# A hybrid attention and DeltaNet layer on one core: new prices for the kernel's own instruction order, decay columns in two products, squares summed by TensorE, softmax sums by transposes

## The chip, the core and the metric

The kernel runs on one core of a Trainium2 chip. The core has five engines with a queue each, executed in order: TensorE (PE; its weight loads are shown apart as PEld), VectorE (DVE), ScalarE (ACT), GpSimd (POOL) and SyncE (SP), which here only issues DMA transfers. The metric is the device time of one execution in microseconds (us).

## The reference

One layer of a diffusion backbone over 512 latent tokens and 256 context tokens of width 1024, in float32:

```python
mod = silu(c) @ w_ada + b_ada                    # 6 x 1024: shift, scale, gate, twice
mod_c = silu(c_ctx) @ w_ada + b_ada              # the same for the context
h  = rms_norm(x, g_norm1) * (1 + sc1) + sh1      # 512 x 1024
hc = rms_norm(ctx, g_norm1) * (1 + csc1) + csh1  # 256 x 1024
aq, ak, av, dq, dk, dv, dz, da, db, ga, gd = split_cols(h @ w_in)   # and of hc @ w_in
y_attn = window_ctx_attention(...)               # 8 heads, window 128, all context keys, a sink
beta = sigmoid(db); g = -exp(a_log) * softplus(da + dt_bias)        # decay columns
o_d = bidir_delta(...)                           # gated DeltaNet, both directions, chunks of 64
y = sigmoid(ga) * (y_attn @ w_br_attn) + sigmoid(gd) * (norm(o_d) * silu(dz) @ w_br_dn)
x = x + gt1 * (y @ w_out)
x = x + gt2 * (square(relu((rms_norm(x, g_norm2) * (1 + sc2) + sh2) @ w_mlp1)) @ w_mlp2)
```

## The kernel before

Channels lie on the 128 partitions and tokens in the free dimension. A float32 product of good accuracy is made of three fast ones: each operand is split into an upper part (rounded by an ACT copy, line 279 for weights and 211 or 308 for features) and the rest (a DVE subtraction, lines 284, 212, 309), and `mm3` issues upper x upper, upper x rest and rest x upper (lines 301, 302, 303); `gate_tiles` does the same on line 1048, and the MLP on line 1517. A weight tile is 128 output columns of all 1024 inputs, 512 KB, in eight k-parts.

**The early stage.** TensorE first runs 30 warm-up products (`NONES`, line 217). x and ctx are loaded whole. `ada(kt)` loads two 512 KB blocks of modulation weights and multiplies them with the condition (line 236, 32 columns wide on the array); `columns(kt)` turns the rows into per-channel scale and shift (lines 252, 257, 265, 266). `norm1` squares x on ACT (line 327), sums four tiles on DVE (lines 333 and 337) and multiplies the sum by ones (line 340) to get the norm; `features(kt)` applies norm, scale and shift (lines 307 to 309), for x and ctx together. Three input tiles, T_AB (the decay columns `da` and `db`: 64 columns that are used, 64 of zeros), T_DK and T_DK + 1, are held in PSUM and fed k by k as the features come; `columns` runs two k ahead (`AHEAD`).

**The rest.** The decay columns become per-chunk decay factors (lines 705 to 763; first used by the products of line 742). Attention has eight units (block of queries, kv head): `scores`, then `outputs`, which transposes the probabilities (line 621), multiplies by the values (lines 610 and 611) and scales with the reciprocal sums, spread over partitions by four f32 products with the identity (line 642). The DeltaNet inverts 32 x 32 blocks on DVE, combines them (lines 893 to 904) and runs a chain of chunk steps in both directions (`chain_step`, lines 1164, 1183, 1203, 1221), whose products use 64 x 64 quadrants of the array. Gate tiles (line 1048) and branch tiles (line 1094) are emitted between as fill. The MLP takes the second half of the time.

**The order.** What is emitted isn't the order of execution. `arrange` takes all instructions with their dependencies (`needs`) and simulates the engines: an engine that is free takes, of the instructions that are ready, the one emitted first. The simulated order is then fixed for every engine, DMA issues on SP and POOL among them. `Step.cost` gives the time that an operation holds its engine and the time until its result is there; `SIGNAL`, 120 ns, is added for a consumer on another engine.

Of the kernel before, what the change touches and what calls it, by code (L numbers as in the profile page):

```python
# [30 lines left out]
AHEAD = 2  # L31
# [5 lines left out]
SIGNAL = 120  # L37
# [30 lines left out]
T_AK, T_AV, T_AQ, T_AB = 0, 1, 2, 6  # L68
T_DK, T_DV, T_DQ, T_DZ = 7, 11, 15, 19
T_GA, T_GD = 23, 31  # L70
N_IN = 39
# [44 lines left out]
def tile_layer(ctx: ExitStack, tc: tile.TileContext, I: dict, out: bass.AP, dbg=None):  # L116
# [25 lines left out]

    def cload(key, shape, pool=const):
        t = pool.tile(list(shape), F32, name=f"c_{key}")
        nc.sync.dma_start(out=t, in_=I[key])
        return t
# [11 lines left out]
    ties = []  # L158

# [46 lines left out]
    def follow(later, earlier):  # L206

        tie(later.ins, earlier.ins.name)
# [19 lines left out]
    def ada(kt):  # L228


        rp_ = banks.get(512, True)
        for half in range(2):
            wb = alloc(1024)
            nc.sync.dma_start(out=wb.ap, in_=I["wada1"][kt, half])
# [3 lines left out]
            wb.free()  # L238
        return rp_
# [47 lines left out]
    early, EARLY = [], {T_AB: 0, T_DK: 0, T_DK + 1: 0}  # L287
    ebufs = []

    def load_early():  # L290
        bb = alloc(1024), alloc(1024)
        ebufs.extend(bb)
        early.append((wload(I["win"][list(EARLY)[len(early)]], bufs=bb), bank(2)))


    def mm3(acc, w, xs, start=True, stop=True, ks=None):
        ks = list(range(len(xs))) if ks is None else ks
        n = len(ks)
        for i, k in enumerate(ks):
            xhi, xlo = xs[i]  # L300
            PE.matmul(acc, w[0][:, k, :], xhi, start=(start and i == 0), stop=False)  # L301
            PE.matmul(acc, w[0][:, k, :], xlo, start=False, stop=False)  # L302
            r = PE.matmul(acc, w[1][:, k, :], xhi, start=False, stop=(stop and i == n - 1))  # L303
        return r
# [10 lines left out]
    w0 = upper[0]  # L315
# [33 lines left out]
    def features(kt):  # L349

        t = alloc(768)
        o, oc = kt * 1024, kt * 512
        if len(hx) == kt:
            hx.append(modulate(t[:, :512], xt[kt], rx, modA[:, kt, 0:1], modS[:, kt, 0:1],
                               H[:, o:o + 512], H[:, o + 512:o + 1024]))
        if len(normed) == 2:
            hc.append(modulate(t[:, 512:768], ct_[kt], rc, modA[:, kt, 1:2], modS[:, kt, 1:2],
                               HCb[:, oc:oc + 256], HCb[:, oc + 256:oc + 512]))
        t.free()
# [5 lines left out]
    normed = [norm1(xs_, 4, SEQ, rx)]  # L365
    follow(w0, normed[0])
    columns(0, rp0)
    features(0)
    hi0 = upper[0]
    columns(1, ada(1))  # L370
    load_early()
    low0 = early_x(*early[0], 0)
    follow(low0, last[0])
    last[0] = low0
    normed.append(norm1(cs_, 2, CTX, rc, hi0))
    for kt in range(KT):
        features(kt)
        if kt + AHEAD < KT:
            columns(kt + AHEAD, ada(kt + AHEAD))
        if len(early) < len(EARLY):  # L380
            load_early()
        for (w, acc), k0 in zip(early, EARLY.values()):
            for k in range(kt + 1) if kt == k0 else (kt,):
                if k or acc is not early[0][1]:
                    early_x(w, acc, k)
                mm3(acc[:, 512:768], w, [hc[k]], start=(k == 0), stop=(k == KT - 1), ks=[k])
# [10 lines left out]
    nc.sync.dma_start(out=mt.ap, in_=I["masks"])  # L397
# [4 lines left out]
    nc.sync.dma_start(out=cost, in_=I["cost"])  # L402
    nc.sync.dma_start(out=sint, in_=I["sint"])
# [193 lines left out]
    def outputs(qb, kv):  # L597
# [43 lines left out]
        for j in range(4):  # L641
            PE.matmul(rb[:, j * P:(j + 1) * P], st[:, 2, j:j + 1].broadcast_to([P, P]), ident, start=True, stop=True)
# [62 lines left out]
    V.tensor_scalar(ad, acc[0:16, :TOK], dtb[0:16], None, op0=ALU.add)  # L705
    V.tensor_scalar(mx, ad, 0.0, None, op0=ALU.max)
    act(be, acc[32:48, :TOK], AF.Exp, scale=-1.0)
    acc.free()
# [948 lines left out]
class Step:  # L1657
# [3 lines left out]
    def __init__(self, ins):  # L1661
        self.name, self.ins, self.kind = ins.name, ins, type(ins).__name__
        self.eng = str(ins.engine).split(".")[-1]
        outs, ins_ = ([o for o in os if getattr(o, "bass_ap", None) is not None] for os in (ins.outs, ins.ins))
        self.writes, self.reads = (sorted({c for o in os for c in self.cells(o.bass_ap)}) for os in (outs, ins_))
        both = [o.bass_ap for o in outs + ins_]
        shared = [c for c in self.reads if c[0] == "bank"]
        self.writes, self.reads = self.writes + shared, [c for c in self.reads if c not in shared]
        self.tiles = {a.tensor.name: a.tensor.manual_sbuf_range for a in both}
        size = lambda a: int(np.prod([n for _, n in a.ap[1:]]))  # L1670
        self.cols = max([size(a) for a in both], default=1)
        self.bytes = max([4 * a.ap[0][1] * size(a) for a in both], default=0)
        self.psum = any(o.bass_ap.tensor.name.startswith("banks") for o in ins_)
        if self.kind == "InstMatmult":
            self.tile, self.cols, self.dtype = tuple(ins.tile_size), size(outs[0].bass_ap), str(ins_[0].dtype)

# [17 lines left out]
    def cost(self):  # L1694

        n = self.cols
        if self.kind == "InstMatmult":
            if self.dtype.endswith("32r"):
                return max(60, 7 + .43 * n if n < 512 else 226), 300
            if self.dtype.endswith("16"):  # L1700
                return 60, 200
            if self.tile == (P, P):
                return max(60, 110 if n <= P else 1.68 * n), 400
            return (142 if self.tile[0] == P else 42 if self.tile[1] > HC else 20), 250
        if self.kind == "InstStreamTranspose":
            return 2010, 2100
        if self.eng == "DVE":
            own = 67 + 1.04 * n + 60 * self.psum if n > 8 else 100
            return own, own + 85
        if self.eng == "Activation":  # L1710
            own = 1290 if "Load" in self.kind else max(195, 36 + .893 * n) + 20 * self.psum
            return own, own + 130
        return 550, 560


def needs(steps, ties):
# [13 lines left out]
    for tag, ts in rings.items():  # L1730
        for old, new in zip(ts, ts[Step.RINGS[tag]:]):
            before[users[new][0]].update(users[old])
    places = {}
# [31 lines left out]

def arrange(tc, nc, ties):

    steps = [Step(i) for i in nc.cur_bb.bb.instructions if "Boundary" not in type(i).__name__]
    before = needs(steps, ties)
    after, left, ready = [[] for _ in before], [len(b) for b in before], [0.] * len(before)  # L1770
# [3 lines left out]
    engines = {"PE", "DVE", "Activation", "Pool", "SP"}  # L1774
    free, links = dict.fromkeys(engines, 0.), {"SP": 0., "Pool": 0.}
    coming, here, last = {e: [] for e in engines}, {e: [] for e in engines}, {}

    def release(ns, at_):
        for n in ns:
            ready[n] = max(ready[n], at_(n))  # L1780
            left[n] -= 1
            if not left[n]:
                if n < len(steps):
                    heapq.heappush(coming[steps[n].eng], (ready[n], n))
                else:
                    release(after[n], lambda _: ready[n])

    first = [n for n, b in enumerate(before) if not b]
    for n in first:
        left[n] = 1  # L1790
    release(first, lambda _: 0.)
    order = mybir.DependencyInfo(mybir.DependencyClass.NoSync, mybir.DependencyReason.DATA)
    for _ in steps:
# [3 lines left out]
        k = heapq.heappop(here[e])  # L1797
        s = steps[k]
        if "DMA" in s.kind:
            rate, lag = (400., 1000) if e == "SP" else (159., 900)  # L1800
            links[e] = max(t + lag, links[e]) + s.bytes / rate
            own, end = (350 if e == "SP" else 900), links[e] + 1300
        else:
            own, end = s.cost()
            end += t
        free[e] = t + own
        own_ = "DMA" not in s.kind

        def seen(n):
            same = own_ and n < len(steps) and steps[n].eng == e  # L1810
            return free[e] if same and e == "PE" else end + 20 if same else end + SIGNAL

        release(after[k], seen)
        if e in last:
            tc.add_manual_dep(s.ins, last[e], order, reason="order")
        last[e] = s.name

# [37 lines left out]
def pack(i):  # L1855
# [24 lines left out]
    ab = np.concatenate([da, z16, db, z16, np.zeros((D, 64), np.float32)], 1)  # L1880
    a["win"] = blk(np.concatenate([ak, av, aqp, ab, dk, dv, dq, dz, ga, gd], 1))
# [16 lines left out]
    prm[0:16, 112] = i["dt_bias"][0].reshape(-1)  # L1898
# [30 lines left out]
```

## Time and profile before

| | us |
|---|---|
| median of 3 runs | 916.5 (915.28 to 919.17) |
| profiled execution, its own time | 918.01 |
| span of the profiled execution | 916.2 |
| mean granted TensorE clock in it | 0.981 of full speed |
| TensorE's largest groups: lines 301, 302, 303 | 212.0, 211.0, 211.2 |
| line 1517 (MLP) | 123.1 |
| line 1048 (gates) with upper and rest weights | 109.2 and 66.1 |

A row of groups names line, engine, operation, tiles and shape, count, then busy us and mean ns of one, then idle time before it. A row of the timeline begins with start and duration in us; neighbours of one kind are merged. Matmuls overlap in the array, so the duration of a record is longer than the distance to the next start, and that distance is what a product costs in a row of products. An f32 product of full precision leaves two records, the fast forms and transposes one.

### The profile page before, as it was taken

To read this page: it belongs to the slowest core of one execution; us is meant where nothing else is said; L and a number is where in the kernel's file an instruction comes from. 1 tells how busy PE (TensorE), PEld (TensorE's weight loads), DVE (VectorE), ACT (ScalarE), POOL (GpSimd) and SP (SyncE) were. 2 spreads that over 40 slices of the span, in tenths; PEclk is the share of its full clock that TensorE was granted. 3 is DMA by queue.
4 is the path that set the end of the run, shared out by engine and by line. 5 is a ranking of instruction groups with operands and counts; after the bars stand their busy time and mean duration, and the time that the engine had idled before them with its cause. 6 is when DMAs were issued, how large, how long until landed. Compare 5 with 4: busy or idle time off the path is not lost.

```text
span 916.2 us, 18029 instructions
## 1 busy us (share of the span) xinstructions
PE 881.1 (96%) x7564; PEld 730.5 (80%) x7564; DVE 652.0 (71%) x1111; ACT 498.8 (54%) x881; POOL 26.1 (3%) x42
## 2 busy tenths in 40 slices
PE   8999999988999998999989999999999999999898
PEld 6688778866777676766768789888898899889886
DVE  5665799966678999667567868896677567737631
ACT  6368774575667896486553434563365246414530
POOL 0000010010000001100000000000000000000000
PEclk9999999999999999899979999999999999999999
DMA  9824356432110236623133645543412332333031
GB/s 351 315 95 93 73 133 140 103 85 47 35 35 24 70 109 215 210 87 101 59 117 128 201 143 185 180 141 115 137 48 93 115 116 69 116 102 129 1 114 47
DMA packets 31985, 107.13 MB, mean 117 GB/s; under 512 B 4000, under 2 KB 4512, under 8 KB 31904
## 3 DMA queue, kind: packets, MB, share of 16 engines
q1 hardware_dynamic: 29600, 97.59, 31.7%
q0 software_dynamic: 2304, 8.39, 5.6%
q8 instruction: 59, 0.97, 0.4%
q14 instruction: 22, 0.18, 0.1%
HBM read 103.87 MB, written 2.10 MB: 116 GB/s over the span
## 4 chain that ended last, share of the span: by engine, by line
PE 82%; ACT 6%; DVE 6%; DMA 3%; issue 2%; SPq 0%; DVEq 0%; ACTq 0%
PE banks L302 14%; PE banks L301 14%; PE banks L303 14%; PE banks L1517 12%; PE banks L1048 10%; PE banks L1094 3%; PE banks L621 2%; DMA m<-in_wada 1%; PE banks L1164 1%; PE banks L684 1%; ACT m L172 1%; DVE m L212 1%; PE banks L236 1%; PE banks L1203 1%; ACT m L211 1%
## 5 line engine op out<-in xcount | busy, mean ns | idle before, releaser
L301 PE MATMUL banks<-m,wh 128*128 128x512 f32 (+1 forms) x568 | 212.0, 374 | 0.6 <-ACT wh L279 0.4
L303 PE MATMUL banks<-m,wl 128*128 128x512 f32 (+1 forms) x568 | 211.2, 372 | 0.0
L302 PE MATMUL banks<-m,wh 128*128 128x512 f32 (+1 forms) x568 | 211.0, 371 | 0.1
L279 ACT ACTIVATE wh<-wr 128x1024 fp32r<-128x1024 f32 (+1 forms) x92 | 90.2, 984 | 146.5 <-PE banks L302 105.3
L1517 PE MATMUL banks<-m,m 128*128 128x256 f32 x1008 | 123.1, 283 | 3.9 <-ACT m L211 3.2
L1517 PEld LDWEIGHTS banks<-m,m 128*128 128x128 f32 x1008 | 122.0, 191 | 5.2 <-ACT m L211 3.6
L301 PEld LDWEIGHTS banks<-m,wh 128*128 128x128 f32 x568 | 107.3, 189 | 19.7 <-ACT wh L279 0.9
L211 ACT ACTIVATE m<-m 128x512 fp32r<-128x512 f32 (+2 forms) x118 | 82.3, 720 | 74.5 <-PE banks L1517 22.5
L303 PEld LDWEIGHTS banks<-m,wl 128*128 128x128 f32 x568 | 107.1, 188 | 18.3 <-issue 0.7
L302 PEld LDWEIGHTS banks<-m,wh 128*128 128x128 f32 x568 | 107.2, 189 | 18.1 <-DVE m L212 0.5
L1048 PE MATMUL banks<-m,wh 128*128 128x512 f32 x320 | 109.2, 416 | 2.4 <-ACT m L172 1.7
L212 DVE TENSOR_TENSOR m<-m,m 128x512 fp32r<-128x512 f32 (+2 forms) x118 | 92.3, 804 | 19.7 <-ACT m L211 13.0
L284 DVE TENSOR_TENSOR wl<-wr,wh 128x1024 fp32r<-128x1024 f32 (+1 forms) x76 | 84.3, 1110 | 13.0 <-ACT wh L279 10.6
L1644 DVE SCALAR_TENSOR_TENSOR m<-banks,modT,m 128x512 f32<-128x512 f32 x32 | 24.0, 750 | 74.4 <-PE banks L303 74.2
L1048 PEld LDWEIGHTS banks<-m,wh 128*128 128x128 f32 x320 | 60.0, 193 | 15.7 <-ACT m L172 2.1
L1048 PE MATMUL banks<-m,wl 128*128 128x512 f32 x160 | 66.1, 414 | 0.0
L302 PE MATMUL banks<-m,m 128*128 128x256 f32 (+1 forms) x136 | 47.1, 348 | 0.7 <-DVE m L309 0.7
L301 PE MATMUL banks<-m,m 128*128 128x512 f32 (+1 forms) x136 | 45.4, 345 | 1.0 <-ACT m L308 1.0
L303 PE MATMUL banks<-m,m 128*128 128x256 f32 (+1 forms) x136 | 45.7, 339 | 0.0
L1113 DVE SCALAR_TENSOR_TENSOR m<-m,m 128x1024 f32<-128x1024 f32 x32 | 38.5, 1221 | 1.7 <-DMA m<-in_wada 1.6
L1048 PEld LDWEIGHTS banks<-m,wl 128*128 128x128 f32 x160 | 30.8, 193 | 7.0
L577 DVE TENSOR_REDUCE st<-banks 128x1 f32<-128x640 f32 (+1 forms) x24 | 22.9, 956 | 14.6 <-PE banks L553 12.2
(258 smaller groups left out, 1362.6 us busy)
## 6 DMA issues: line engine op xcount, KB each, us to landing
m<-in_wada SPq DMA_DIRECT2D x48, 512.0 KB, 5.2
wr<-in_wm SPq DMA_DIRECT2D x40, 512.0 KB, 3.6
wr<-in_win SPq DMA_DIRECT2D x39, 512.0 KB, 3.6
m<-in_wm SPq DMA_DIRECT2D x24, 512.0 KB, 3.6
wl<-in_win POOLq DMA_DIRECT2D x16, 512.0 KB, 5.8
m<-in_xT SPq DMA_DIRECT2D x8, 512.0 KB, 5.2
wr<-in_wbr SPq DMA_DIRECT2D x16, 256.0 KB, 2.6
wr<-in_wout SPq DMA_DIRECT2D x8, 512.0 KB, 4.0
```

Of the source, the lines that this page charges most:

```text
L211: A.activation(r32(hi), src, AF.Copy)
L212: (eng or V).tensor_tensor(r32(lo), src, hi, op=ALU.subtract)
L279: upper[0] = A.activation(r32(hi), raw, AF.Copy)
L284: V.tensor_tensor(r32(lo), raw, hi, op=ALU.subtract)
L301: PE.matmul(acc, w[0][:, k, :], xhi, start=(start and i == 0), stop=False)
L302: PE.matmul(acc, w[0][:, k, :], xlo, start=False, stop=False)
L303: r = PE.matmul(acc, w[1][:, k, :], xhi, start=False, stop=(stop and i == n - 1))
L1048: PE.matmul(acc.ap, w[x][:, k, :], hx[k][y], start=(k == p == 0), stop=(k == KT - 1 and p == 2))
L1094: PE.matmul(pa.ap, w[x][:, j, :], r32(Q[y][:, :, j, :]), start=(j == p == 0), stop=(j == 3 and p == 2))
L1113: V.scalar_tensor_tensor(wa.ap, wa.ap, 0.5, scr.ap, op0=ALU.mult, op1=ALU.mult, accum_out=modT[:, grp, j:j + 1])
L1517: PE.matmul(dst, r32(self.w[w][i][:, k * P:(k + 1) * P]), xs7[x][k][j], start=(n == 0), stop=(n == 11))
L1644: V.scalar_tensor_tensor(xn_[ct], accs[ct].ap, modT[:, 3, ct:ct + 1], xn_[ct], op0=ALU.mult, op1=ALU.add)
```

## The change

It has five parts.

- The 64 decay columns get an array of their own, `wab`. Upper parts fill columns 0 to 63 of the weight and the rest columns 64 to 127, so that two products per k (the weight with upper and rest of the features) replace three; the two halves of the result are added afterwards.
- The sum of squares of x: the four tiles' squares are folded to 512 columns each and added up by four products with ones in PSUM. Half of the last square is made on DVE.
- The early stage is emitted in another sequence: all modulation products and columns before the remaining features, context features apart, and constants are loaded after the last modulation weights.
- Line 642's products become transposes.
- The prices of `arrange` and its rule: other costs per operation, a signal price per consuming engine (34 to 60 ns), a limit of eight SP transfers in flight, a model of TensorE's instruction fetch, a price for going between whole-array and quadrant products, and `STICK`: TensorE keeps to the kind that it is in if such an instruction is ready within 50 places of the first ready one.

```diff
-SIGNAL = 120
+STICK = 50
...
+    def load(out, key, *at):
+        d = nc.sync.dma_start(out=out, in_=I[key][at] if at else I[key])
+        if lastload:
+            tie(d.ins, lastload[0].ins.name)
+        return d
...
+        raw = wp.tile([P, KT, P], F32, tag="wr", bufs=NWR, name=nm("wr"))[:, :4].rearrange("p k (h c) -> p (k h) c", h=2)
+        nc.sync.dma_start(out=raw, in_=I["wab"])
...
+        upper[0] = A.activation(r32(w[:, :, :CH]), raw, AF.Copy)
+        V.tensor_tensor(r32(w[:, :, CH:]), raw, w[:, :, :CH], op=ALU.subtract)
+        return r32(w), None
...
             PE.matmul(acc, w[0][:, k, :], xhi, start=(start and i == 0), stop=False)
-            PE.matmul(acc, w[0][:, k, :], xlo, start=False, stop=False)
-            r = PE.matmul(acc, w[1][:, k, :], xhi, start=False, stop=(stop and i == n - 1))
+            end = stop and i == n - 1
+            r = PE.matmul(acc, w[0][:, k, :], xlo, start=False, stop=(end and w[1] is None))
+            if w[1] is not None:
+                r = PE.matmul(acc, w[1][:, k, :], xhi, start=False, stop=end)
...
+    def norm_x():
+        ss = bank()
+        for i in range(4):
+            b = alloc(1024)
+            src = xs_[:, i * 1024:(i + 1) * 1024]
+            n = 512 if i == 3 else 1024
+            A.activation(b[:, :n], src[:, :n], AF.Square)
+            if i == 3:
+                V.tensor_tensor(b[:, n:], src[:, n:], src[:, n:], op=ALU.mult)
+            V.tensor_tensor(b[:, :512], b[:, :512], b[:, 512:], op=ALU.add)
+            PE.matmul(ss.ap, ones, b[:, :512], start=(i == 0), stop=(i == 3))
...
+    rp1 = ada(1)
+    load_early()
+    norm_x()
     columns(0, rp0)
     features(0)
...
+    early_x(*early[0], 0)
+    columns(1, rp1)
+    features(1)
+    columns(2, ada(2))
     load_early()
...
+    norm1(cs_, 2, CTX, rc)
+    for kt in range(3, KT):
+        columns(kt, ada(kt))
     for kt in range(KT):
...
+        if kt > 1:
+            features(kt)
+        features_c(kt)
+        for n, e in enumerate(early):
+            if kt > 1 or n == 2:
+                early_x(*e, kt)
+            early_c(*e, kt)
...
-            PE.matmul(rb[:, j * P:(j + 1) * P], st[:, 2, j:j + 1].broadcast_to([P, P]), ident, start=True, stop=True)
+            PE.transpose(rb[:, j * P:(j + 1) * P], st[:, 2, j:j + 1].broadcast_to([P, P]), ident)
...
-    V.tensor_scalar(ad, acc[0:16, :TOK], dtb[0:16], None, op0=ALU.add)
+    ab = t2[64:128]
+    A.activation(t2[0:64], acc[64:128, :TOK], AF.Copy)
+    V.tensor_tensor(ab, t2[0:64], acc[0:64, :TOK], op=ALU.add)
+    acc.free()
+    V.tensor_scalar(ad, ab[0:16], dtb[64:80], None, op0=ALU.add)
...
+SEEN = {"PE": 54, "DVE": 34, "Activation": 37, "Pool": 60, "SP": 60}
...
+        if e == "PE":
+            same = min((x for x in here[e] if steps[x].whole == whole), default=k)
+            if same <= k + stick:
+                k = same
...
+            if len(flight) >= 8:
+                t = max(t, flight[-8])
...
+                t = max(t, asked.get(int(had / 256 - .6), 0))
+                if s.whole != whole:
+                    t += 92 if whole else 130
```

More of the change, by code (lines that the diff above doesn't have):

```diff
@@ L233, in ada @@
             wb = alloc(1024)
-            nc.sync.dma_start(out=wb.ap, in_=I["wada1"][kt, half])
+            d = load(wb.ap, "wada1", kt, half)
             for g in range(4):
@@ L238, in ada @@
             wb.free()
+        if kt == KT - 1:
+            lastload.append(d)
         return rp_
@@ L396, in tile_layer @@
     mt = alloc(256)
-    nc.sync.dma_start(out=mt.ap, in_=I["masks"])
+    load(mt.ap, "masks")
     V.tensor_copy(maskb, mt.ap.rearrange("p (d k) -> p d k", d=2))
@@ L1673, in __init__ @@
         self.psum = any(o.bass_ap.tensor.name.startswith("banks") for o in ins_)
-        if self.kind == "InstMatmult":
+        self.dma = "DMA" in self.kind
+        self.whole = self.kind != "InstMatmult"
+        if not self.whole:
             self.tile, self.cols, self.dtype = tuple(ins.tile_size), size(outs[0].bass_ap), str(ins_[0].dtype)
+            self.whole = self.tile == (P, P)
     @staticmethod
@@ L1732, in needs @@
             before[users[new][0]].update(users[old])
+        for old, new in zip(ts, ts[1:]):
+            before[users[new][0]].add(users[old][0])
     places = {}
@@ L1769, in arrange, with listed @@
     before = needs(steps, ties)
+    order = mybir.DependencyInfo(mybir.DependencyClass.NoSync, mybir.DependencyReason.DATA)
+    last = {}
+    for k in listed(steps, before):
+        s = steps[k]
+        if s.eng in last:
+            tc.add_manual_dep(s.ins, last[s.eng], order, reason="order")
+        last[s.eng] = s.name
+def listed(steps, before, stick=STICK):
+    n = len(steps)
     after, left, ready = [[] for _ in before], [len(b) for b in before], [0.] * len(before)
@@ L1773, in arrange, with release @@
             after[p].append(k)
[L1774 to L1784, printed above, removed]
-                else:
[L1786 to L1790, printed above, removed]
+    engines = ("PE", "DVE", "Activation", "Pool", "SP")
+    free, links = dict.fromkeys(engines, 0.), {"SP": 3200., "Pool": 0.}
+    free["SP"] = 750.
+    coming, here, out = {e: [] for e in engines}, {e: [] for e in engines}, []
+    flight, whole, cold = [], True, False
+    words, asked = 0, {n: 0. for n in range(3)}
+    def release(ks, at_):
+        for k in ks:
+            ready[k] = max(ready[k], at_(k))
+            left[k] -= 1
+            if not left[k]:
+                if k < n:
+                    heapq.heappush(coming[steps[k].eng], (ready[k], k))
+                else:
+                    release(after[k], lambda _: ready[k])
+    first = [k for k, b in enumerate(before) if not b]
+    for k in first:
+        left[k] = 1
     release(first, lambda _: 0.)
-    order = mybir.DependencyInfo(mybir.DependencyClass.NoSync, mybir.DependencyReason.DATA)
     for _ in steps:
@@ L1796, in arrange @@
             heapq.heappush(here[e], heapq.heappop(coming[e])[1])
-        k = heapq.heappop(here[e])
-        s = steps[k]
[L1799 to L1802, printed above, removed]
-        else:
-            own, end = s.cost()
-            end += t
-        free[e] = t + own
[L1807 to L1811, printed above, removed]
+        k = here[e][0]
@@ L1813, in arrange, with seen @@
+        free[e] = t + own
+        def seen(x):
+            if x >= n:
+                return end + 40
+            f = steps[x].eng
+            if not s.dma and f == e:
+                return free[e] if e == "PE" else end + 10
+            return end + SEEN[f]
         release(after[k], seen)
-        if e in last:
-            tc.add_manual_dep(s.ins, last[e], order, reason="order")
-        last[e] = s.name
+    return out
 def _constants():
```

112 lines of the change are left out of this document (65 added, 47 removed).

## The prediction

> **What bounds the kernel now.** I read the page's totals and its chain of waits first, to find the engine that sets the end.
>
> ```profile
> span 916.2 us, 18029 instructions
> PE 881.1 (96%) x7564; PEld 730.5 (80%) x7564; DVE 652.0 (71%) x1111; ACT 498.8 (54%) x881; POOL 26.1 (3%) x42
> PE 82%; ACT 6%; DVE 6%; DMA 3%; issue 2%; SPq 0%; DVEq 0%; ACTq 0%
> ```
>
> TensorE is on the path for 82%, so a matmul taken away usually counts and one on another engine usually does not. A busy TensorE need not be a fast one, so next comes the view of windows: per stretch the length, the busy time of PE, PEld, DVE, ACT and POOL, then the granted clock, the DMA share and GB/s.
>
> ```profile
> 15.00:40.00 25.00, 22.57 (x142) 13.50 (x141) 16.46 (x31) 11.62 (x20) 0.00 (x0) 0.86 1.02 385
> 40.00:60.00 20.00, 20.00 (x147) 15.76 (x146) 14.58 (x30) 8.38 (x14) 0.74 (x1) 1.00 0.44 148
> 60.00:180.00 120.00, 119.01 (x1012) 97.18 (x1011) 100.04 (x201) 83.32 (x132) 10.39 (x12) 1.00 0.46 102
> 180.00:300.00 120.00, 109.70 (x874) 88.90 (x872) 86.69 (x146) 82.25 (x153) 6.40 (x9) 0.97 0.22 47
> 400.00:460.00 60.00, 59.35 (x994) 41.27 (x992) 37.16 (x79) 39.00 (x126) 0.00 (x0) 1.00 0.27 84
> 460.00:481.00 21.00, 16.72 (x322) 12.63 (x319) 13.99 (x34) 12.67 (x37) 0.00 (x0) 0.67 0.37 127
> 600.00:917.00 317.00, 308.44 (x1829) 274.74 (x1827) 197.91 (x275) 129.42 (x166) 0.00 (x0) 1.00 0.29 95
> ```
>
> From 40 to 180 us and from 600 us on TensorE is full at full clock: only less work helps, and the MLP at the end (no edit changes its work) keeps its length. Time lies in three places. Between 15 and 40 us DMA is saturated, TensorE is idle for 25.00 - 22.57 = 2.4 us, and clock 0.86 costs 25 x 0.14 = 3.5 us more: 5.9. In attention (180 to 300) it is 10.3 idle and 120 x 0.03 = 3.6 of clock: 13.9. At the tail of the latent DeltaNet chain (460 to 481) it is 4.3 idle and 21 x 0.33 = 6.9 of clock: 11.2. From 400 to 460 TensorE never rests, yet the timeline shows what it loses there (start, duration, both in us):
>
> ```profile
> 400.86 0.61 PE L1048 MATMUL banks<-m,wh 128*128 128x512 f32 x2
> 401.41 0.46 PE L1203 MATMUL banks<-m,m 64*64 64x64 f32 x16
> 401.80 0.73 PE L1048 MATMUL banks<-m,wl 128*128 128x512 f32 x2
> 402.37 0.62 PE L1048 MATMUL banks<-m,wh 128*128 128x512 f32 x2
> ```
>
> A row of two whole-array products takes 0.61 to 0.62, but 0.73 right after a quadrant group; starts there are 0.23 apart otherwise, so the two from 400.86 should have made room at 401.32 and L1203 came at 401.41. Add the way back (0.39 for 16 products of some 0.02 each) and a round trip between whole-array and quadrant products costs about 0.3 us beside its work.
>
> **The change, part by part.** The sum is made against this execution: 918.0 us with a span of 916.2. The shown runs' median, 916.5, is 1.5 lower, which I take off at the end.
>
> *Decay columns in two passes.* The tile T_AB had upper and lower weights in three products per k; now both halves share one 128-column weight and two products suffice. Removed: 8 products of 512 columns and 8 of 256.
>
> ```profile
> 31.37 0.40 PE L301 MATMUL banks<-m,m 128*128 128x512 f32 x1
> 31.61 0.40 PE L302 MATMUL banks<-m,m 128*128 128x512 f32 x1
> 32.07 0.28 PE L301 MATMUL banks<-m,m 128*128 128x256 f32 x1
> 32.19 0.28 PE L302 MATMUL banks<-m,m 128*128 128x256 f32 x1
> ```
>
> Starts are 0.23 and 0.12 apart, so 8 x 0.35 = 2.8 us go, in the stretch from 20 to 60 us; TensorE is full in its second half, so I count all. Bounds: 1.4 if half lands in the starved part, 2.8. The load shrinks from 512 to 256 KB, 0.7 us of link at the 385 GB/s of the second window. Added behind the tile: one ACT copy of 64 rows x 768 and one DVE add.
>
> ```profile
> 59.63 1.00 DVE L705 TENSOR_SCALAR m<-banks,c_prm 16x768 f32<-16x768 f32 x1 [2.97 <-PE banks L303]
> 69.37 0.60 DVE L715 TENSOR_SCALAR m<-m,nega 16x768 f32<-16x768 f32 x1
> 78.52 1.52 PE banks L742 x48
> ```
>
> L705 prices each at 1.0, ACT's copy by its nearest neighbour. The result is ready at 69.97 and first used at 78.5: 8.5 us of room for 2.0, while TensorE works on other tiles (119.01 of 120 busy). Cost zero; without that cover, 2.0.
>
> *Softmax sums by transposes.* Line 642 spreads the reciprocal sums with 32 f32 products of 128 columns; now they are transposes.
>
> ```profile
> L621 PE MATMUL banks<-c_ident,m 128*128 128x128 f32 x144 | 21.7, 274 | 3.2 <-ACT m L172 2.2 <-DVE m L636 1.0
> L642 PE MATMUL banks<-c_ident,st 128*128 128x128 f32 x64 | 8.6, 274 | 0.0
> 179.64 0.87 PE banks L621 x8
> 190.23 0.89 PE banks L642 x8
> ```
>
> Lines 621's 144 transposes leave 144 records, line 642's 32 products leave 64, and a record costs 0.11 in both. So 32 x 0.11 = 3.5 us of TensorE go, in a stage that is 109.7 of 120 busy: bounds 0 and 3.5, I take 2.5.
>
> [...] The rows: from 180 to 300 us, with L621's transposes in it, the clock was 0.97. [...]
>
> *Squares summed by TensorE, products first, constants later.* Lines 333 and 337 summed four tiles on DVE before one product; now each tile's folded squares go to TensorE.
>
> ```profile
> 1.07 9.46 PE L217 MATMUL banks<-ones 128*128 128x128 f32 x60 [1.07 <-DVE ones L182]
> 9.47 1.06 ACT L327 ACTIVATE m<-m 128x1024 f32<-128x1024 f32 x1 [0.16 <-DMA m<-in_xT]
> 12.87 1.10 PE L340 MATMUL banks<-m,ones 128*128 128x512 f32 x2 [0.20 <-DVE m L337]
> 14.42 0.28 DVE L265 TENSOR_SCALAR modA<-banks,bada,c_prm 128x2 f32<-128x2 f32 x1 [1.69 <-PE banks L257]
> 15.39 0.75 DVE L307 SCALAR_TENSOR_TENSOR m<-m,modA,m 128x512 f32<-128x512 f32 x1 [0.56 <-ACT m L172]
> 299.48 0.86 PE banks L684 x2
> 14.46 0.33 SPq L145 DMA_DIRECT2D c_ident<-in_ident  x1
> 20.83 0.33 SPq L145 DMA_DIRECT2D c_nmask<-in_nmask  x1
> 22.13 3.28 SPq L234 DMA_DIRECT2D m<-in_wada  x4
> ```
>
> A product of this kind costs 0.86 (L684), and the warm-up of L217 holds TensorE until 10.53, so four end at 13.97 at the earliest if they queue behind it: just where L340 ended. If the warm-up is out of the way, the last needs only the last square, at half size until 10.0 (L327 at 1.06 for twice as much), a fold of 512 columns on DVE, at L307's 0.75, and 0.86: about 11.6. But L307 also needs the modulation columns of 14.42, so it starts at 14.8 at best, against 15.39: -0.6; at worst the modulation products queue behind the four squares and it comes 1 us later. I take zero. The reorder hands every modulation product to TensorE as its weights land and puts the constant loads, five of which SP issued from 14.46 to 21.2 ahead of the next weights at 22.13, behind the last of them; L742, the first to use c_selq among them, runs at 78.5. The features then exist earlier and fill the 5.9 us lost between 15 and 40. Bounds +1 and -5.9; I take -2.5.
>
> *Prices and stickiness.* The order on all engines is drawn up from these prices, so this part moves everything up to 480 us. The old signal price is 120 ns per hop between engines on top of the tail of the operation. Two rows late in the chain show what a hop takes:
>
> ```profile
> 467.36 0.42 DVE L1214 TENSOR_TENSOR m<-m,banks 128x256 f32<-128x256 f32 x1 [0.51 <-PE banks L1203]
> 467.83 0.71 PE L1221 MATMUL banks<-m,m 64*64 64x64 f32 x16 [0.59 <-DVE m L1214]
> ```
>
> TensorE starts 0.05 after DVE's end, so the old order holds back chain steps by 0.1 per hop, runs gate products ahead in their place and has none left at 460. With 54 ns the fill is spread further: of the 11.2 us in the tail I take 3 (bounds 0 and 11.2), of attention's 13.9 I take 1 (bounds +4 and -7, since half of it stays with softmax's own latencies). Stickiness saves round trips:
>
> ```profile
> L1164 PE MATMUL banks<-m,m 64*64 64x64 f32 x608 | 15.3, 234 | 0.4 <-DVE m L1228 0.2
> L1183 PE MATMUL banks<-m,m 64*64 64x64 f32 x384 | 11.2, 235 | 3.2 <-DVE m L1169 2.7 <-ACT m L936 0.4
> L1203 PE MATMUL banks<-m,m 64*64 64x64 f32 x352 | 11.2, 230 | 0.9 <-ACT m L1195 0.9
> L1221 PE MATMUL banks<-m,m 64*64 64x64 f32 x256 | 9.6, 253 | 0.9 <-DVE m L1214 0.6 <-ACT m L1195 0.2
> ```
>
> In groups of 32 (L1164) and 16 these are 19 + 24 + 22 + 16 = 81 groups, 24 us at 0.3 each. Joining both directions' groups would halve that; where they are a hop apart it can't. I take 4, bounds 0 and 12.
>
> Sum: -2.8 - 2.5 - 2.5 - 3 - 1 - 4 = -15.8; 918.0 becomes 902.2, and less 1.5 about **901 us**.
>
> **Rivals.**
>
> *The order is worth nothing* (chance 0.18). Only the decay columns count; transposes save time in which TensorE waits anyway, and the new order loses as much as it gains. For it: attention's idle time sits behind ACT and DVE (the releasers in L621's row). Against: between 400 and 460 nothing but switching is lost. 918.0 - 2.8 - 1.5 = 914.
>
> *The half-clock stretches go* (0.17). If the early stage and the tail run without gaps, their 5.9 and 11.2 vanish whole: 918.0 - 2.8 - 3.5 - 5.9 - 11.2 - 4 - 4 - 1.5 = 885 (attention 4). For it: both have idle time and low clock together. Against: the tail is a chain of hops, and its fill is a fixed number of products.
>
> *Stickiness starves the chain* (0.15), the slower side. A ready chain group waits while whole products within 50 places are issued. One direction's latent chain has 8 steps with 4 groups, 32 in a row; two more products of 0.23 ahead of each make 32 x 0.46 = 14.7 us, the fill is gone sooner, and nothing hides the tail. 918.0 + 14.7 - 2.8 - 2.5 - 1.5 = 926. For it: in the old order TensorE is never idle from 400 to 460, so fill is always at hand. It decides from 0.3 us a group: 32 x 0.3 = 9.6 outweighs the removed work by 4.3.
>
> [...]
>
> **How the numbers follow.** The forecast has 0.50; its own range has all terms at half, 909, and the order's (2.5, 3, 1, 4) doubled, 890. To hold 8 in 10 the range takes in the second rival's 885 and the first's 914 with some of the slow side: 884 to 919. A difference of 0.5%, 4.6 us, is what can be told from none. Faster (below 911.9): 0.48 of the forecast, the 0.17, and 0.05 of the first rival, 0.70. Within: 0.02, 0.13 and 0.02 of the slow one, 0.17. Slower: 0.13.
>
> **What would show it.** Right: the records of lines 621 and 642 with one per transpose; 16 products fewer in the early tile; clock above 0.86 between 15 and 40; fewer row changes between gate and quadrant products from 380 to 480, and gate products until the chain's last steps; the MLP as long as before, shifted. Wrong: chain steps further apart than the 10 us of now, new half-clock stretches in attention, or a first feature much after 15.39.

## The result and the profile after

The changed kernel took 907.32 us (median of 4 runs, 906.8 to 908.95) against 916.22 in the same session: 8.9 us less, a ratio of 0.990 with an interval of 0.9875 to 0.9926. The prediction was 901 with a range of 884 to 919. The profiled execution took 906.80 us.

The page of the changed kernel, its span, totals and instruction queue:

```profile
span 905.0 us, 17951 instructions
PE 873.4 (97%) x7522; PEld 719.8 (80%) x7522; DVE 651.7 (72%) x1113; ACT 497.8 (55%) x882; POOL 26.1 (3%) x42
q8 instruction: 59, 0.97, 0.4%
```

TensorE is 7.7 us less busy, the other engines are as before. The instruction queue (packets, MB, share) brought 59 blocks in both kernels. The profiled execution of the kernel before took 918.01 us, 1.8 above its median, so the spans differ by 11.2 us where the medians differ by 8.9. To find where the 11.2 went I take four points that both kernels have, from the views of single lines (start of the first and the last instruction). Before, then after:

```profile
L742 PE MATMUL banks<-c_selq,m x48: 226/226/247, 78.4 to 79.8; 64*64 64x40 f32 x48
L621 PE MATMUL banks<-c_ident,m x144: 270/273/332, 179.5 to 283.4; 128*128 128x128 f32 x144
L904 PE MATMUL banks<-m,m x192: 191/191/212, 201.3 to 374.0; 32*32 32x32 f32 x192
L1221 PE MATMUL banks<-m,m x256: 218/218/366, 403.2 to 477.0; 64*64 64x64 f32 x128
```

```profile
L792 PE MATMUL banks<-c_selq,m x48: 226/226/247, 75.0 to 76.3; 64*64 64x40 f32 x48
L668 PE MATMUL banks<-c_ident,m x144: 270/272/422, 174.3 to 274.7; 128*128 128x128 f32 x144
L954 PE MATMUL banks<-m,m x192: 191/194/258, 192.0 to 369.2; 32*32 32x32 f32 x192
L1271 PE MATMUL banks<-m,m x256: 218/218/366, 397.7 to 464.5; 64*64 64x64 f32 x128
```

Differences of the last starts, stage by stage:

| stage, up to | before | after | gained in the stage |
|---|---|---|---|
| decay columns (742 / 792) | 79.8 | 76.3 | 3.5 |
| end of attention (621 / 668) | 283.4 | 274.7 | 5.2 |
| end of the block combination (904 / 954) | 374.0 | 369.2 | -3.9 |
| end of the chain (1221 / 1271) | 477.0 | 464.5 | 7.7 |
| end of the span | 916.2 | 905.0 | -1.3 |

The windows of the changed kernel (length, busy PE, PEld, DVE, ACT, POOL, clock, DMA share, GB/s) show the same three places as before, and a fourth, the block combination, which the prediction had left out:

```profile
15.00:40.00 25.00, 22.14 (x192) 14.00 (x185) 19.51 (x43) 15.15 (x28) 1.47 (x2) 1.00 0.98 393
174.00:275.00 101.00, 94.95 (x773) 73.44 (x772) 71.57 (x118) 68.81 (x125) 6.41 (x9) 0.98 0.23 51
334.00:367.00 33.00, 27.46 (x512) 21.50 (x511) 25.73 (x32) 17.40 (x29) 3.87 (x8) 0.84 0.64 225
398.00:465.00 67.00, 65.53 (x1271) 45.05 (x1262) 43.82 (x100) 43.46 (x147) 0.00 (x0) 0.97 0.25 80
440.00:465.00 25.00, 24.73 (x504) 16.85 (x495) 17.10 (x42) 15.99 (x53) 0.00 (x0) 1.00 0.20 63
465.00:481.00 16.00, 14.80 (x72) 12.17 (x73) 14.76 (x26) 9.10 (x15) 0.00 (x0) 1.00 0.43 153
```

and the block combination in the kernel before:

```profile
344.00:375.00 31.00, 26.34 (x618) 20.54 (x617) 23.90 (x29) 17.54 (x32) 4.88 (x10) 0.89 0.59 201
```

The early stage is at full clock (0.86 before). The chain's last 25 us have gate products still at hand, at full clock, where the tail before stood at 0.67. But the block combination is idle for 5.5 us of 33 at clock 0.84; before, it was 4.7 of 31 at 0.89. The view of waits of the changed kernel (who waited for whom: us in total, times, longest) names what TensorE waits for there:

```profile
PE banks L943 <- issue: 2.6, 1, 2.6
PE banks L954 <- issue: 2.3, 1, 2.3
PE banks L617 <- ACT m L180: 2.0, 1, 2.0
...
PE banks L953 <- issue: 0.6, 1, 0.6
```

and of the kernel before:

```profile
PE banks L904 <- issue: 4.0, 1, 4.0
...
PE banks L893 <- issue: 0.5, 1, 0.5
```

"Issue" means that the profile shows nothing that TensorE waited for. I take it that it had no instructions; the times of the instruction blocks bear that out (TensorE went on 1.2 to 1.5 us after one had moved, last section). Lines 943, 953 and 954, and lines 893 and 904 before, are the tiny products that combine inverted blocks. Line 617, in the changed kernel, is a score product in attention that waits for a softmax exponential.

### The profile page after: what moved, and what is told of

Its sections match the earlier page's. It is cut to its first block, busy times and chain, and to the rows that moved or that the text cites. A ratio compares the mean times of both kernels' runs of the same rounds, so it can differ in the third digit from the quotient of the medians.

```text
span 905.0 us, 17951 instructions
## 1 busy us (share of the span) xinstructions
PE 873.4 (97%) x7522; PEld 719.8 (80%) x7522; DVE 651.7 (72%) x1113; ACT 497.8 (55%) x882; POOL 26.1 (3%) x42
## 4 chain that ended last, share of the span: by engine, by line
PE 49%; DVE 3%; DMA 2%; ACT 1%; issue 0%; DVEq 0%; SPq 0%
PE banks L1567 12%; PE banks L327 10%; PE banks L329 10%; PE banks L325 10%; PE banks L1098 5%; DVE m L220 1%; DMA m<-in_wm 1%; PE banks L1214 1%; DMA m<-in_wada 1%; PE banks L1253 1%; DVE m L333 1%; PE banks L1233 1%; DVE m L335 1%; ACT m L219 1%; DVE m L1163 0%; PE banks L1271 0%
## 5 line engine op out<-in xcount | busy, mean ns | idle before, releaser
L329 PE MATMUL banks<-m,m 128*128 128x512 f32 (+1 forms) x120 | 39.6, 334 | 0.0
L180 ACT ACTIVATE m<-banks,st 128x512 f32<-128x512 f32 (+1 forms) x32 | 23.5, 737 | 15.5 <-DVE st L625 15.4
```

The lines of the kernel that those rows point to most:

```text
L180: r = A.activation(out_, in_, func, **kw)
L329: r = PE.matmul(acc, w[1][:, k, :], xhi, start=False, stop=end)
```

## The experiments

The theory: both halves of the change help, the order by about twice what the removed work gives, through the signal price (the chain) and through stickiness. The rival: removed work and early sequence make all of it. Ratios are against runs of the kernel before in the same session, their medians were 915.2 to 916.2.

### The two halves apart

`b_prices` is the kernel before with the new `Step`, `needs`, `arrange` and `listed`; `a_oldprices` is the changed kernel with the old ones.

```diff
-SIGNAL = 120
+STICK = 50
...
+SEEN = {"PE": 54, "DVE": 34, "Activation": 37, "Pool": 60, "SP": 60}
...
+def listed(steps, before, stick=STICK):
...
```

> The kernel before with the new prices, the new rule and nothing else. If the gain of the changed kernel is made by the order (theory), the chain of chunk steps ends sooner here too: its stage is some 6 us shorter, and the run comes to 908 to 912 us. If the order is worth nothing and the removed products make the gain (rival), it stays at 914 to 918.

> The changed kernel with the old prices and the old rule. By the theory that the order makes two thirds of the gain, 912 to 915 us: 3.6 us of TensorE work less and the early stage as changed, but the chain's tail at half clock again. By the rival that the removed work and the early sequence make all of it, 906 to 909.

Measured: `b_prices` 897.44 us, ratio 0.9789 (0.9761 to 0.9817), far past what I expected and 10 us faster than the whole change. `a_oldprices` 913.77, ratio 0.9969 (0.995 to 0.9988). So the prices alone give 2.1%, the other edits alone 0.3%, and the two together 1.0%: on top of the new prices, edits that take work from TensorE cost 10 us. Under the old prices the transposes alone gave 3.9 us (below), so that the decay columns, the squares and the new sequence together gave nothing there that the intervals show. The same four points of `b_prices`:

```profile
L742 PE MATMUL banks<-c_selq,m x48: 226/226/247, 77.5 to 78.9; 64*64 64x40 f32 x48
L621 PE MATMUL banks<-c_ident,m x144: 270/272/330, 177.4 to 274.7; 128*128 128x128 f32 x144
L904 PE MATMUL banks<-m,m x192: 184/191/212, 195.1 to 362.4; 32*32 32x32 f32 x192
L1221 PE MATMUL banks<-m,m x256: 218/218/267, 390.9 to 455.8; 64*64 64x64 f32 x128
...
PE banks L904 <- issue: 1.7, 1, 1.7
```

Attention's last transpose starts at 274.7 in both, though the changed kernel began its first one 3.1 us earlier (174.3 against 177.4). In the block combination `b_prices` gains 6.8 us on the changed kernel (362.4 against 369.2, with 1.7 us of waiting for instructions against 5.5), in the chain 1.9 more.

The clock is a part of this that I had not followed. The mean granted clock of single executions was 0.976 to 0.989 in 60 of the kernel before (median 0.984), 0.982 to 0.986 in the changed kernel, and 0.995 to 0.997 in `b_prices`. An estimate from these: span times the missing share is 14.6, 13.6 and 4.0 us, an upper bound since it counts idle time too. By it some 11 of the 19 us that the prices gain, and nearly all of the 10 that the changed kernel loses to `b_prices`, is time at half clock. Executions of one kernel follow the clock too (the kernel before took 912.20 us at 0.987 and 922.42 at 0.977). How much of the order's worth is clock is not shown, since no run changes the clock alone.

### The signal price and stickiness

```diff
-SEEN = {"PE": 54, "DVE": 34, "Activation": 37, "Pool": 60, "SP": 60}
+SEEN = dict.fromkeys(("PE", "DVE", "Activation", "Pool", "SP"), 120)
```

> The kernel before with the new prices, but 120 ns for a signal to any engine, as of old. If the lower signal price spreads the gate products over the chain (the prediction's mechanism), the chain's tail is empty and at half clock again and the run takes 905 to 912 us. If the gain of the new prices comes from elsewhere (costs, fetch, change of kind), 896 to 900.

Measured: 909.5 us, ratio 0.9934 (0.9912 to 0.9957). The signal price alone takes back 12 of the 19 us. The tail is empty again, in the windows of `bp_sig120`, beside `a_oldprices` below it:

```profile
460.00:481.00 21.00, 17.73 (x227) 14.38 (x226) 16.20 (x32) 10.74 (x27) 0.00 (x0) 0.76 0.44 151
```

```profile
460.00:481.00 21.00, 17.07 (x244) 13.60 (x241) 14.06 (x31) 11.44 (x32) 0.00 (x0) 0.67 0.39 140
```

The gate line (1048) has 2 records between 460 and 470, where the chain ends, against 22 in the last 10 us of the chain of `b_prices`. The chain ends at 469.7 instead of 455.8: of these 13.9 us, 2.6 lie ahead of attention (the last product of line 742 at 81.5 against 78.9, with the early stage at clock 0.80 here), 3.8 in attention, which I had put at 1 us (last transpose at 281.1 against 274.7), and 7.9 in the chain, while the block combination gives back 0.4. The profiled execution took 914.54, the slowest of the twelve, so these stages together are longer than in a median execution.

```diff
-STICK = 50
+STICK = 0
```

> The changed kernel with a stickiness of 0 places. By the prediction's term stickiness saves 4 us of round trips between whole-array and quadrant products, so 910 to 912 us without it. By the rival that it saves nothing (in the chain's stage the trace has 83 changes of kind after the change and 75 before), 906 to 908.5.

Measured, in the changed kernel: 911.17 us, ratio 0.9945 (0.992 to 0.997), so stickiness gives about 4 us, the size that I took; the two intervals just touch. Counted in the records, the changed kernel goes 160 times from one kind of product to the other, without stickiness 180 times: 10 round trips at the 0.3 us that the prediction read from the timeline are 3. But they do not lie in the chain alone (83 against 91 there), and the views of single lines and windows put the loss ahead of it:

```profile
L668 PE MATMUL banks<-c_ident,m x144: 270/273/421, 177.7 to 280.7; 128*128 128x128 f32 x144
L1271 PE MATMUL banks<-m,m x256: 218/218/267, 402.8 to 468.3; 64*64 64x64 f32 x128
...
15.00:40.00 25.00, 23.13 (x166) 13.88 (x166) 17.24 (x37) 11.69 (x23) 1.47 (x2) 0.86 0.97 380
```

Attention ends 6.0 us later than in the changed kernel. But 3.4 of that is there at its first transpose (177.7 against 174.3), behind an early stage that in this execution stood at clock 0.86, and the chain's end is 3.8 later. The size is the one that I took; that the saved round trips make it is not shown.

### The edits one by one

`b_transpose` is the kernel before with the transposes. The old prices are the same for both forms, so that no engine's order changes.

```diff
-            PE.matmul(rb[:, j * P:(j + 1) * P], st[:, 2, j:j + 1].broadcast_to([P, P]), ident, start=True, stop=True)
+            PE.transpose(rb[:, j * P:(j + 1) * P], st[:, 2, j:j + 1].broadcast_to([P, P]), ident)
```

> The kernel before with transposes for the spreading of the softmax sums; the old prices make no difference between the two, so that the order is the same instruction by instruction. If the 3.5 us of TensorE are on the path, 912.5 to 913.5 us; by the prediction's term, 2.5 off, 913.7; if attention waits for other engines there anyway, 915 to 917.

Measured: 912.31 us, ratio 0.9951 (0.993 to 0.9973): 3.9 us less. `bp_transpose` is the same edit on `b_prices`, where the new prices do tell the two forms apart (110 against 220 ns on TensorE):

> The kernel before with the new prices and the transposes. If the transposes save what they do under the old order (3.9 us), 893 to 895 us. If attention under the new order waits for other engines instead, 897 to 899. If it is they that cost the changed kernel its 10 us against the new prices alone (2.4 of them in attention, 5 in the block combination by its trace), 903 to 908.

Measured: 909.88 us, ratio 0.9926 (0.9901 to 0.9951). The edit that saves 3.9 us under the old prices costs 12.4 under the new. `bp_decay` is `b_prices` with the decay columns in two products, all else of the early sequence as before:

```diff
-    ab = np.concatenate([da, z16, db, z16, np.zeros((D, 64), np.float32)], 1)
+    ab = np.concatenate([da, z16, db, z16], 1)
+    a["wab"] = np.ascontiguousarray(ab.reshape(KT, P, 64).transpose(1, 0, 2))
...
+            if w[1] is not None:
+                r = PE.matmul(acc, w[1][:, k, :], xhi, start=False, stop=end)
```

> The kernel before with the new prices and the decay columns in two products, the early sequence as before. If the removed 2.8 us of TensorE are on the path, 894 to 896 us. If any shift of the early stage disturbs the later order, 900 to 908.

Measured: 896.34 us, ratio 0.9797 (0.9763 to 0.9832): 1.1 us less than `b_prices` by the medians, a little more by the ratios, so that the two can't be told apart. They are the fastest kernels of the study, 2.0% below the kernel before and some 1% below the changed one. The sum of squares, `a_norm1`, is the changed kernel with the old sum:

```diff
-    norm_x()
+    norm1(xs_, 4, SEQ, rx)
```

> The changed kernel with the squares of x summed on DVE and one product, as before. The first feature came 1.6 us later after the change (16.99 against 15.39), behind the four products. If the sum by TensorE is what the early stage loses, the decay columns are read 1 to 3 us earlier and the run takes 904 to 906 us. If the four products keep the clock up between 15 and 40 us (1.00 after the change, 0.86 before), a half-clock stretch returns there and it takes 908 to 911.

Measured: 908.58 us, ratio 0.9918 (0.9887 to 0.9949): no difference from the changed kernel that the intervals show. Its line 776, the counterpart of 742, starts at 77.0 against 75.0; but that point moved by 2.2 us between `before` and `b_transpose` too (78.4 and 76.2), whose instructions are the same up to there, in the same order. What differed was the clock between 15 and 40 us, 0.86 and 1.00. The early stage can't be settled to within 2 us by one profile each.

### Is it the transposes or the order they draw?

Two kernels keep the one and change the other. In `bp_tr_asprod` the chip runs transposes, in the order of `b_prices`; in `bp_prod_astr` it runs products, in the order of `bp_transpose`. The price has two parts, the cost and the instruction words that the model of the fetch counts; both are exchanged.

```diff
+        self.tr = not self.whole and self.ins.is_transpose and not any(t.split("_")[0] == "st" for t in self.tiles)
...
-                return (110, 280) if self.ins.is_transpose else (max(62, 1.72 * n), max(62, 1.72 * n) + 170)
+                return (110, 280) if self.tr else (max(62, 1.72 * n), max(62, 1.72 * n) + 170)
...
-                one = s.dtype.endswith("32r") or s.dtype.endswith("16") or s.ins.is_transpose
+                one = s.dtype.endswith("32r") or s.dtype.endswith("16") or s.tr
```

> The kernel before with the new prices and the transposes, but with the transposes of the softmax sums priced as the products were, so that every engine's order is that of b_prices (897.4 us). If the order drawn from the transposes' own price cost bp_transpose its 12 us, 893 to 898 us. If the transposes cost the time by what they do on the chip (a colder clock, a longer wait), 906 to 911 again.

> The counterpart: the kernel before with the new prices, products as before, priced as transposes, so that every engine's order is that of bp_transpose (909.9 us). If the order is the cause, 910 to 914 us: that of bp_transpose, and up to 3.5 us for the dearer products. If the transposes on the chip are the cause, 897 to 901.

Measured: `bp_prod_astr` 909.87 us, ratio 0.9932 (0.9914 to 0.9949). With no transpose in place of a product it is as slow as `bp_transpose`, 12.4 us above `b_prices`: the order alone does that. Its waits, and where attention ends:

```profile
PE banks L903 <- issue: 3.4, 1, 3.4
...
PE banks L1183 <- ACT m L936: 2.1, 3, 1.3
PE banks L570 <- ACT m L172: 2.0, 1, 2.0
```

```profile
L621 PE MATMUL banks<-c_ident,m x144: 270/272/422, 177.0 to 281.4; 128*128 128x128 f32 x144
```

Line 570 is line 617 of the changed kernel: the same score product waits 2.0 us for a softmax exponential in both, and 0.2 in `b_prices`. Attention ends 6.7 us later than there.

`bp_tr_asprod` took 903.93 us, ratio 0.9857 (0.9831 to 0.9883), between the two expectations: the order of `b_prices`, 3.5 us less work on TensorE, and 6.5 us slower. Its profile says where:

```profile
L621 PE MATMUL banks<-c_ident,m x144: 270/273/332, 177.1 to 274.1; 128*128 128x128 f32 x144
L904 PE MATMUL banks<-m,m x192: 184/191/212, 194.8 to 367.8; 32*32 32x32 f32 x192
```

```profile
PE banks L894 <- issue: 5.2, 1, 5.2
...
PE banks L904 <- issue: 1.6, 2, 1.0
```

Attention starts 0.3 us and ends 0.6 us earlier than in `b_prices`: the 3.5 us that transposes save are worth 0.3 there. Then TensorE waits 5.2 and 1.6 us for instructions in the block combination, against 1.7, which is later by 5.4 at its end. The trace has the times at which the blocks of instructions moved (start and duration in us, bytes):

```
b_prices       340.14 0.92 16384   348.13 0.96 16384   353.74 1.01 16384   358.42 0.96 16384
bp_tr_asprod   344.32 1.96 16384   351.95 0.96 16384   356.95 0.96 16384
```

In `b_prices` TensorE stood from 348.7 to 350.4, 1.3 us past the end of the block of 348.13; in `bp_tr_asprod` from 349.0 to 354.2, 1.3 us past the block of 351.95. Meanwhile, from 346 to 355 us, transfers moved 360 GB/s in `b_prices` and 338 in `bp_tr_asprod`. A transpose leaves half the records of a product (32 transposes 32 in the changed kernel, 32 products 64 before), so I take it that the same tiny products lie elsewhere in their block of instructions. That this shift is what makes the wait 5.2 instead of 1.7 is argued from these times; no run moved the boundary alone. Four pairs of kernels have the same order with products and with transposes, and in them the times follow the waits (one profile each):

| products, transposes | time, us | difference | waits for "issue", us |
|---|---|---|---|
| `before`, `b_transpose` | 916.17, 912.31 | -3.9 | 4.5, 4.1 |
| `bp_prod_astr`, `bp_transpose` | 909.87, 909.88 | 0.0 | 4.4, 5.8 |
| `bp_decay`, `bp_decay_tr_asprod` (below) | 896.34, 900.85 | 4.5 | 3.8, 6.2 |
| `b_prices`, `bp_tr_asprod` | 897.44, 903.93 | 6.5 | 1.7, 6.8 |

So a shift need not make the waits longer; where it didn't, the transposes paid.

The blocks here have 16,384 bytes, 59 of them 0.97 MB; how many TensorE holds no run here shows.

The same price on the changed kernel and on the kernel with decay columns and transposes:

> The changed kernel with nothing altered but the price of the softmax sums' transposes, set to that of the products they replace. If that price drew the order that costs the changed kernel its 10 us against b_prices, 893 to 900 us. If the new early sequence and the four sums of squares cost them, 905 to 909 as it is.

> The kernel before with the new prices, the decay columns in two products and the transposes, these priced as products: the order of bp_decay (896.3 us) with 3.5 us less TensorE work. If the order is the cause, 892 to 896 us, the fastest so far. If the transposes on the chip are, 905 to 910.

Measured: `a_tr_asprod` 902.44 us, ratio 0.9853 (0.9827 to 0.988), and `bp_decay_tr_asprod` 900.85, ratio 0.9835 (0.9813 to 0.9857). Both lie between their expectations as `bp_tr_asprod` does. In the first, attention's last transpose starts at 271.4 against 274.7, and instructions are waited for longer than in the changed kernel:

```profile
PE banks L943 <- issue: 4.4, 1, 4.4
...
PE banks L953 <- issue: 2.2, 2, 1.3
```

So of the 10 us between the changed kernel and `b_prices`, 5 go back to a price for 32 transposes. The cause of the other 5 stays open. Waiting for instructions (6.6 us against 1.7) is as large, but it doesn't settle them: the profiled execution, the fastest of the six, has these waits and took 897.91, as long as `b_prices`, while the six range up to 907.03, with granted clocks from 0.995 down to 0.987.

## Why the prediction was right, and where it was not

The sign and the range were right, the size was not: 15.8 us forecast, 8.9 measured. The step that failed is the adding of the parts. Prices and stickiness had 8 us and gave 18.7 alone; the other edits had 7.8 and cost 9.9 on top of them. That the sum came near all the same is luck: two errors of opposite sign met.

- **Decay columns, 2.8 us.** The 16 products went as forecast. What they give in time stays open: under the new prices the medians differ by 1.1 us and the ratios the other way. (The 385 GB/s in its working are those of the first window shown, 15 to 40 us.)
- **Transposes, 2.5 us.** Right in place (the records halve, the line's busy time fell from 8.6 to 5.3 us, and the kernel gained 3.9 under the old order), and within the prediction's own bounds of 0 and 3.5 in attention under the new (0.3). What failed is that the term was added to the order's: the price of the transposes is part of the order, and it cost 12 us on the new prices. That transposes by themselves lower the clock, the profiles don't show: in the same order the granted clock of attention was the same with products and with transposes, 0.97 and 0.97 (`bp_prod_astr`, `bp_transpose`), 1.00 and 1.00 (`b_prices`, `bp_tr_asprod`).
- **Early stage, 2.5 us.** Too much. The clock was 1.00 between 15 and 40 us as hoped, and line 792 came 3.5 us earlier, where both early terms together have 5.3. But the sequence doesn't make this clock: `b_prices` and `b_transpose`, without it, had 1.00 as well, and `a_nostick`, with it, 0.86.

```profile
15.00:40.00 25.00, 21.75 (x171) 14.59 (x171) 19.16 (x40) 13.36 (x23) 0.00 (x0) 1.00 1.01 398
...
15.00:40.00 25.00, 22.90 (x159) 14.76 (x159) 18.43 (x37) 13.42 (x24) 0.00 (x0) 1.00 1.00 386
```

  An estimate at like clocks: line 742 or 792 starts at 76.2 (`b_transpose`), 75.0 (changed) and 73.4 (`a_oldprices`) at clock 1.00, at 78.4 (before) and 76.8 (`a_nostick`) at 0.86, so that both terms are worth some 1.2 to 2.8 us there. The first feature came at 16.99, 1.6 later, past the bound of +1, which the prediction had named as a sign of being wrong: the modulation products queued behind the squares as feared. Their second half started at 14.76 instead of 12.03, behind the fourth square, and the columns' copy followed at 15.46 instead of 12.73.

- **Signal price, 3 + 1 us.** Mechanism right: fill lasts until the chain ends, and 120 ns brings the empty tail back. Size wrong: 12 us. In the one profile the chain has 7.9 of it for 3 and attention 3.8 for 1, where I had said of the 13.9 us that half "stays with softmax's own latencies".
- **Stickiness, 4 us.** Measured 3.9, but the mechanism failed: the fewer changes of kind that the prediction named as a sign did not come. The chain had 75 before and has 83 after.
- **The MLP unchanged.** It ends 1.3 us later after the chain in the changed kernel, 440.5 against 439.2 before; not followed further.
- **Block combination.** The prediction had no term for it. It lost 3.9 us, and the wait for instructions, 4.5 us in the profile of before, went unread.

Of the rivals, the half-clock stretches did go from the early stage and the chain's tail in the profile of the changed kernel, but those of the block combination stayed (0.89 before, 0.84 after), and the rival's 885 was not reached by any version. Its mechanism counts all the same: `b_prices`, far ahead, is also the kernel with hardly any time at half clock (4.0 us at most, by the estimate above). Stickiness did not starve the chain. That the order is worth nothing is refuted.

## What to carry to other kernels

Where a program draws its order from prices, the gain of an edit under one set of prices says nothing of its gain under another: measure each edit on the prices that it will live with, and keep the order fixed (by pricing the new operation as the old) to tell the operation from the order it draws. Price a hop between engines from pairs of rows in the trace; here 120 ns in place of 34 to 60 decided more than all the removed products. Look for the blocks of instructions behind "issue" waits in stretches of tiny products: here TensorE went on 1.2 to 1.5 us after a block had moved, and in one order the waits were 1.7 us with products and 6.8 with transposes. And before two profiles are compared stage by stage, compare their granted clocks: here the same instructions reached line 742 2.2 us apart, at 0.86 and 1.00 between 15 and 40 us.

## What the runs showed of the hardware

TensorE stood still for 0.5 to 5.2 us at a time, without a semaphore to wait for. In the fourteen profiles this happened 34 times, 29 of them in streams of 32 x 32 products, and each time TensorE went on 1.2 to 1.5 us after a 16 KB block of instructions had moved; the sum of these waits was between 1.7 and 8.7 us in kernels with nearly the same work. In the kernel before, the wait of 4.0 us ended at 363.66, 1.3 after the end of the block of 361.40 (0.96 us long).

The granted clock of these profiles is 1.00 or 0.50 and changes in steps of 3.41 us. Two places of the kernel before (length, busy PE, PEld, DVE, ACT and POOL, clock, DMA share, GB/s):

```profile
16.57:19.98 3.41, 1.91 (x18) 0.69 (x18) 2.79 (x3) 2.23 (x3) 0.00 (x0) 1.00 1.03 414
19.98:26.81 6.83, 6.35 (x34) 2.94 (x26) 5.09 (x11) 2.80 (x5) 0.00 (x0) 0.50 1.02 329
463.71:467.12 3.41, 0.99 (x32) 0.84 (x32) 2.55 (x6) 1.61 (x7) 0.00 (x0) 1.00 0.27 77
467.12:480.78 13.66, 11.94 (x190) 9.25 (x186) 8.58 (x21) 7.56 (x24) 0.00 (x0) 0.50 0.47 167
```

Worked out for all fourteen, up to 890 us: whenever the clock fell to 0.50, TensorE had been busy for at most 2.3 us of the 3.41 before. A stretch at full clock that was busier than that was never followed by half clock; one with 1.8 to 2.3 was followed by either. In the first stretch above TensorE was idle for 1.5 us in sum before the clock fell; `b_transpose`, with the same instructions, was busy for 2.1 us in its stretch up to 20.1 and kept its clock. What decides between them is not shown.

In the one stretch of the timeline before that the prediction shows, the quadrant products of 401.41 came 0.09 us later than the row ahead of them made room (401.32). Going back cost about 0.1, an estimate: of the 0.39 up to 401.80, the 16 products take some 0.26 at the 0.016 between their starts. The row of two whole-array products after it took 0.73 instead of 0.62, 0.11 more.
